# Feed-forward: T forms and the weights of the 256-column products at other columns, with one low block per run placed 64 bytes ahead

## The chip, the cores and the metric

The kernel runs on one core of a Trainium2 chip. The metric is the device time of one execution in microseconds (us). All inputs start in the chip's memory and the output ends there.

## What is computed

The reference is a two-layer encoder trunk in float32 on x of 512 x 1024. Each layer has a mixer (attention in layer 0, mLSTM in layer 1), a memory cross-attention and a gated feed-forward; a last RMS norm follows. The change touches the feed-forward alone:

```python
def conv_ffn(xn, w_up, conv_w, conv_b, w_down):
    h = causal_depthwise_conv(xn @ w_up, conv_w) + conv_b
    g, u = jnp.split(h, 2, axis=-1)
    return (jax.nn.gelu(g) * u) @ w_down
```

`w_up` is 1024 x 5632 and `w_down` 2816 x 1024. `w_up` is cut into 22 pairs of 128-column blocks: block p of g and block p of u.

## The kernel before, in words

**Three products for one.** Every float32 operand is split into a high part (rounded to the format that TensorE multiplies at full rate) and a low part (what is left). `mm3` (L271) forms one product as three matmuls into one bank: low-by-high of the moving side last. In the profile L274 is wh by xh, L275 is wh by xl, and L276 is wl by xh. The high part is made by ScalarE (`scalar.copy`), the low part by VectorE (`sub`, L264 and L265, a subtraction raw minus high).

**The feed-forward** (`ffn_steps`) goes through the 22 pairs. Pairs 0 to 3 (`plain`, L1290) use 512-column matmuls: 8 blocks of the contraction for g, 8 for u. Pairs 4 to 21 (`seven`, L1309) use a Strassen-Winograd scheme: the two halves of the contraction, the two halves of the 512 tokens and the pair's two blocks make a 2 x 2 by 2 x 2 product, done in seven products of 4 contraction blocks and 256 columns each instead of eight. Three of them (p1, p2, p3) take columns of the normal input x as the moving operand: the **X products**. Four (p4 to p7) take sums of x that are formed once per layer in `forms` (L1222) and kept split in the tiles th0 to th3 and tl0 to tl3 (L1216): the **T forms**, and the **T products**. A product is 4 blocks x 3 matmuls = 12 matmuls. The two layers have 36 such pairs, so 36 x 84 = 3024 matmuls of 256 columns, 1296 of them with X and 1728 with T.

The weights of the seven products are f3 (1024 columns, for p1 and p2), f1 (1024, for p5 and p7), s2 (512, p6), s4 (512, p3) and a22 (512, p4). `split` (L1331) makes their parts: one copy on ScalarE, one subtraction on VectorE. f1 and f3 take tiles wh and wl of 1088 columns from a rotating pool (`parts`, L251); f3 starts OFF = 16 columns, or 64 bytes, into its tile. s2, s4 and a22 have tiles of their own. Unused tiles (`pad`) push others on: 192 bytes ahead of the T forms (L1215), 64 bytes ahead of s4 (L1328).

**Where the operands lie.** All operands start at a multiple of 64 bytes. The question of this case is whether that multiple is even (a multiple of 128 bytes) or odd (64 bytes past one). In the addresses that the program before assigns, with the moving operand named first and the weights second: X products (even, odd), T products (odd, even), all 512-column products (even, even).

**The order of the work.** A small list scheduler (`Sched`, L141) holds one queue for each engine. Tasks carry a duration, dependencies, slots and a due time; the scheduler replays them and calls their functions in its order, which is the order in which the instructions are issued; a framework below it may still interleave neighbouring tasks. PE's order puts the seven products in the order p1, p6, p5, p2, p7, p3, p4, and between them, through `fill` (L1424), blocks of the second matrix (`down`, L1411): 12 matmuls of 512 columns, two or so for each pair. A **run** below means consecutive 256-column products with no 512-column block between them.

VectorE makes in each pair the low parts, two sums of weights (L1340, L1346), five sums of products (L1380), one scaling (L1401), four convolution taps (L1263), the gated product (L1273) and the addition of a down block to x (L495).

Of the kernel before, what the change touches and what calls it, by code (L numbers as in the profile page):

```python
# [10 lines left out]
F32R = mybir.dt.float32r  # L11
# [5 lines left out]
P = 128  # L17
# [19 lines left out]
OFF = 16  # L37
# [24 lines left out]
class Plan:  # L62
# [70 lines left out]
class Task:  # L133
    def __init__(self, eng, dur, fn, deps, prio, take, free, lat):
# [2 lines left out]
        self.take, self.free = take, free  # L137
        self.end = None


class Sched:  # L141

# [20 lines left out]
    def run(self):  # L163
        order = sorted(self.tasks, key=lambda t: (t.prio, t.n))
# [7 lines left out]
        now = {e: 0.0 for e in todo}  # L172
        inf = float("inf")
        idle = 0.0
        while any(todo.values()):
            best = None
            for e, ts in todo.items():
# [34 lines left out]
                st["_" + r] = s  # L212
            for r, st in t.free:
                self.slots[r][st["_" + r]] = t.end + 0.1
            if t.fn:
                t.fn()
        self.now, self.idle = now, idle


class Builder:  # L220
# [22 lines left out]
    def bank(self, tag):  # L243
        tag, bufs = BANKS[tag]
        return self.til(self.aux, tag, bufs=bufs)
# [22 lines left out]
        self.nc.scalar.copy(hi, v)  # L268
        self.sub(lo, v, hi)

    def mm3(self, out, wh, wl, xh, xl, first, last, parts=False):  # L271

        mm = self.nc.tensor.matmul
        mm(out, wh, xh, start=first, stop=False, skip_group_check=parts)  # L274
        mm(out, wh, xl, start=False, stop=False, skip_group_check=parts)  # L275
        mm(out, wl, xh, start=False, stop=last, skip_group_check=parts)  # L276
# [841 lines left out]
    def ffn_steps(self, layer, mp):  # L1118
# [36 lines left out]
        def parts(st, off=0):  # L1155
            st["wh"], st["wl"] = self.parts(off)
# [60 lines left out]
        formed, pads = [], []  # L1217
# [91 lines left out]
        def seven(p, fill):  # L1309
# [14 lines left out]
            l1 = load(a22, "ra", A2[:, 512:], 512, at - 6.0)  # L1324

            def small(s, tag):
                if tag == "s4" and not pads:
                    pads.append(self.pad(mp, 64))  # L1328
                s["wh"], s["wl"] = (self.til(mp, tag + i, (P, 512), F32R, bufs=1) for i in "hl")

            def split(s, cols, deps, due, alloc, take, raw, free=()):  # L1331
                def hi():
                    alloc()
                    nc.scalar.copy(s["wh"][:, :cols], raw())

                h = add("ACT", act(cols), hi, deps, due - 3.0, take)
                return add("DVE", tt(cols), lambda: self.sub(s["wl"][:, :cols], raw(), s["wh"][:, :cols]), [h], due - 2.0, (), free)
# [5 lines left out]
            w3 = split(f3, 1024, [l2], at, lambda: parts(f3, OFF), [("h", f3)], lambda: r2["raw"][:])  # L1343
            w2 = split(s2, 512, [b2], at, lambda: small(s2, "s2"), [("s2", s2)], SB)
            w1 = split(f1, 1024, [b1], at + 1.0, lambda: parts(f1), [("h", f1)], lambda: sa["sa"][:])
            b4 = add("DVE", tt(512), lambda: tt_(out=SB(), in0=SB(), in1=r2["raw"][:, 512:], op=ALU.add), [w2], at - 1.5)  # L1346
            w22 = split(a22, 512, [l1], at + 4.0, lambda: small(a22, "a22"), [("a22", a22)], lambda: a22["ra"][:], [("ra", a22)])
            w4 = split(s4, 512, [b4], at + 5.0, lambda: small(s4, "s4"), [("s4", s4)], SB, [("sb", sb)])
# [19 lines left out]
            p1 = pe(n, lambda: opened("X", bx, "acc", f3, 0, *X(0, 0), "X", True), [w3], [("acc", bx)])  # L1368
            p6 = pe(n, lambda: opened("Y", by, "acc", s2, 0, *T2, "Y", True), [w2, *formed], [("acc", by)], [("s2", s2)])
            p5 = pe(n, lambda: opened("R", br, "s", f1, 512, *T1, "R", True), [w1], [("s", br)])  # L1370
            get = rows(st, at + 2.0)

            def v_():
# [3 lines left out]
            def sum_(tag, out, a, b, op):  # L1377
                if tag:
                    st[tag] = self.til(mp, tag, (P, 256), bufs=1)
                tt_(out=out(), in0=a(), in1=b(), op=op)  # L1380
# [4 lines left out]
            v = add("ACT", act(256), v_, [p1], at + 1.5, [("v", bv)])  # L1385
            u2 = add("DVE", 0.34, lambda: sum_("u2", tmp("u2"), bank("Y"), tmp("v_"), ALU.add), [p6, v], at + 4.0, [("u2", bu2)])
            p2 = pe(n, lambda: product(f3, 512, *X(1, 0), "X", False), [p1, v], (), [("h", f3)])
            c11 = add("ACT", act(256), lambda: nc.scalar.copy(hs(0, 0)(), bank("X")()), [p2, get], clock[0] + 2.0, (), [("acc", bx)])
            p7 = pe(n, lambda: product(f1, 0, *T3, "Y", False), [u2, p5], (), [("h", f1)])
            u3 = add("DVE", 0.34, lambda: sum_("u3", tmp("u3"), bank("Y"), tmp("v_"), ALU.add), [p7], clock[0], [("u3", bu3)])  # L1390
            c22 = add("DVE", 0.34, lambda: sum_(None, hs(1, 1), tmp("u3"), bank("R"), ALU.subtract), [u3, p5, get], clock[0], (), [("u3", bu3)])
            fill()
            p3 = pe(n, lambda: product(s4, 0, *X(1, 1), "R", False), [c22, w4], (), [("s4", s4)])
            c12 = add("DVE", 0.34, lambda: sum_(None, hs(0, 1), bank("R"), tmp("u2"), ALU.subtract), [p3, get], clock[0], (), [("s", br), ("u2", bu2)])
            p4 = pe(n, lambda: product(a22, 0, *T4, "Y", False), [u3, w22], (), [("a22", a22)])
            c21 = add("DVE", 0.34, lambda: sum_(None, hs(1, 0), bank("Y"), tmp("v_"), ALU.add), [p4, get], clock[0], (), [("acc", by), ("v", bv)])
            fill()

# [416 lines left out]
```

## Time and profile before

| | |
|---|---|
| median of 3 executions | 1494.97 us (1494.59 to 1495.11) |
| the profiled execution | 1494.89 us, of which 1493.1 us is the span from the first to the last instruction |
| granted TensorE clock, mean | 0.999 |
| PE, busy | 1480.1 us (99%), 8570 instructions |
| VectorE (DVE), busy | 1209.5 us (81%), 2291 instructions |
| ScalarE (ACT), busy | 815.7 us (55%) |
| first `seven` pairs to the last, layer 0 and layer 1 | about 460 to 716 us and 1181 to 1437 us of the span |

A time in a profile line is in us from the span's start. The start of a matmul is recorded, its end is modelled, so the distance from one start to the next is what counts; "mean ns" of a matmul group is the modelled length from start to end, which is longer than that distance because matmuls overlap in the array.

### The profile page before, as it was taken

How to read it: one execution, taken by the hardware profiler on the slowest of the kernel's cores; microseconds unless marked ns; L12 is line 12 of the kernel's file. 1: busy time of each engine (PE TensorE's matmuls, PEld its weight loads, DVE VectorE, ACT ScalarE, POOL GpSimd, SP SyncE). 2: the span in 40 equal slices, each digit the busy share in tenths (PEclk: the TensorE clock that was granted, in tenths of full speed). 3: DMA queues.
4: the chain of work that ended last, by engine and by line, in shares of the span. 5: the costliest groups of instructions: out<-in, count | busy, mean ns of one | idle time of the engine just before them, and what ended most of it. 6: DMA issues, size and time to landing. Idle time of an engine off the chain costs nothing.

```text
span 1493.1 us, 22741 instructions
## 1 busy us (share of the span) xinstructions
PE 1480.1 (99%) x8570; PEld 1283.7 (86%) x8570; DVE 1209.5 (81%) x2291; ACT 815.7 (55%) x1369; POOL 61.4 (4%) x104
## 2 busy tenths in 40 slices
PE   9999999999999999999999999999999999999998
PEld 7888777888889999999888778888888899999987
DVE  7779795666689999999868857666566999999984
ACT  7777573444466555556446634444444655555654
POOL 0000130000001000000000000000000000000000
PEclk9999999999999999999999999999999999999999
DMA  5212223323237665562222222223323656565422
GB/s 195 85 59 82 86 84 115 127 72 127 81 131 191 168 155 157 148 162 76 91 97 85 71 99 85 99 91 121 114 72 126 179 156 170 153 158 160 108 74 75
DMA packets 62461, 174.92 MB, mean 117 GB/s; under 512 B 6800, under 2 KB 6800, under 8 KB 62352
## 3 DMA queue, kind: packets, MB, share of 16 engines
q1 hardware_dynamic: 56160, 153.48, 31.4%
q0 software_dynamic: 5184, 18.88, 7.5%
q8 instruction: 67, 1.10, 0.3%
q10 hardware_dynamic: 1008, 1.12, 0.2%
q14 instruction: 42, 0.34, 0.1%
HBM read 171.35 MB, written 2.10 MB: 116 GB/s over the span
## 4 chain that ended last, share of the span: by engine, by line
PE 90%; DVE 6%; ACT 2%; issue 1%; DMA 0%; SPq 0%; DVEq 0%; ACTq 0%
PE acc L274 18%; PE acc L276 18%; PE acc L275 18%; PE w L276 5%; PE w L274 5%; PE w L275 5%; PE s L274 3%; PE acc L335 2%; PE s L276 2%; PE acc L337 2%; PE acc L336 2%; PE s L275 2%; PE w L1603 1%; DVE wl L265 1%; PE s L401 1%
## 5 line engine op out<-in xcount | busy, mean ns | idle before, releaser
L274 PE MATMUL acc<-xh,wh 128*128 128x512 f32 (+1 forms) x800 | 285.1, 357 | 0.0
L276 PE MATMUL acc<-xh,wl 128*128 128x512 f32 (+1 forms) x800 | 280.8, 351 | 0.0
L275 PE MATMUL acc<-xl,wh 128*128 128x512 f32 (+1 forms) x800 | 280.5, 351 | 0.0
L265 DVE TENSOR_TENSOR wl<-raw,wh 128x1024 fp32r<-128x1024 f32 (+2 forms) x197 | 235.5, 1195 | 42.9 <-ACT wh L268 39.7
L268 ACT CAST wh<-raw 128x1024 fp32r<-128x1024 f32 (+2 forms) x137 | 140.6, 1029 | 164.0 <-PE acc L275 97.7
L275 PEld LDWEIGHTS acc<-xl,wh 128*128 128x128 f32 x800 | 151.3, 189 | 19.7
L276 PEld LDWEIGHTS acc<-xh,wl 128*128 128x128 f32 x800 | 150.2, 188 | 20.2
L274 PEld LDWEIGHTS acc<-xh,wh 128*128 128x128 f32 x800 | 150.2, 188 | 19.8
L1263 DVE SCALAR_TENSOR_TENSOR c<-hs,vec,c 128x512 f32<-128x512 f32 x176 | 129.7, 745 | 0.5
L274 PE MATMUL w<-ah,wh 128*128 128x512 f32 x304 | 119.1, 392 | 0.2
L276 PE MATMUL w<-ah,wl 128*128 128x512 f32 x304 | 118.7, 390 | 0.3
L275 PE MATMUL w<-al,wh 128*128 128x512 f32 x304 | 118.6, 390 | 0.0
L1256 ACT ACTIVATE c<-hs,vec 128x512 f32<-128x512 f32 x88 | 70.4, 813 | 40.5 <-DVE hs L1401 38.0
L276 PEld LDWEIGHTS w<-ah,wl 128*128 128x128 f32 x304 | 57.1, 188 | 12.7 <-DVE wl L265 0.9
L274 PEld LDWEIGHTS w<-ah,wh 128*128 128x128 f32 x304 | 57.1, 188 | 12.2 <-ACT wh L1165 1.5
L275 PEld LDWEIGHTS w<-al,wh 128*128 128x128 f32 x304 | 57.1, 188 | 10.0
L1165 ACT CAST wh<-dr 128x512 fp32r<-128x512 f32 x64 | 39.6, 618 | 45.3 <-PE acc L275 19.2
L274 PE MATMUL acc<-mem,wh 128*128 128x256 f32 (+1 forms) x192 | 61.5, 320 | 0.0
L276 PE MATMUL acc<-mem,wl 128*128 128x256 f32 (+1 forms) x192 | 61.1, 318 | 0.0
L275 PE MATMUL acc<-mem,wh 128*128 128x256 f32 (+1 forms) x192 | 60.8, 317 | 0.0
L495 DVE TENSOR_TENSOR x<-acc,x 128x512 f32<-128x512 f32 x32 | 22.1, 690 | 46.9 <-PE acc L276 46.9
L495 DVE TENSOR_TENSOR x<-w,x 128x512 f32<-128x512 f32 x72 | 49.2, 683 | 12.6 <-PE w L276 12.5
(373 smaller groups left out, 3948.2 us busy)
## 6 DMA issues: line engine op xcount, KB each, us to landing
raw<-in_up_dram SPq DMA_DIRECT2D x52, 512.0 KB, 3.3
sa<-in_up_dram SPq DMA_DIRECT2D x36, 512.0 KB, 4.1
sa<-in_up_dram POOLq DMA_DIRECT2D x36, 512.0 KB, 5.9
dr<-in_down_dram SPq DMA_DIRECT2D x64, 256.0 KB, 2.9
ra<-in_up_dram SPq DMA_DIRECT2D x36, 256.0 KB, 2.8
raw<-in_xk_dram SPq DMA_DIRECT2D x16, 512.0 KB, 3.4
raw<-in_wo_dram SPq DMA_DIRECT2D x16, 512.0 KB, 3.3
raw<-in_xq_dram SPq DMA_DIRECT2D x16, 512.0 KB, 3.3
```

The lines of the kernel that those rows point to most:

```text
L265: self.nc.vector.tensor_tensor(out=lo, in0=v, in1=hi.bitcast(F32), op=ALU.subtract)
L268: self.nc.scalar.copy(hi, v)
L274: mm(out, wh, xh, start=first, stop=False, skip_group_check=parts)
L275: mm(out, wh, xl, start=False, stop=False, skip_group_check=parts)
L276: mm(out, wl, xh, start=False, stop=last, skip_group_check=parts)
L335: mm(ps, xh[k][:, ts], wh[:, ws], start=(k == 0), stop=False)
L336: mm(ps, xh[k][:, ts], wl[:, ws], start=False, stop=False)
L337: mm(ps, xl[k][:, ts], wh[:, ws], start=False, stop=(k == 7))
L495: self.nc.vector.tensor_tensor(out=self.x[m][:], in0=ps[:], in1=self.x[m][:], op=ALU.add)
L1165: nc.scalar.copy(st["wh"][:, :cols], st[tag][:, :cols])
L1256: nc.scalar.activation(st["c_"][:, j, :], hs()[:, j, 2:514], AF.Identity, scale=self.col("cw", (layer * 3 + 2) * 44 + blk), bias=self.col( ...
L1263: nc.vector.scalar_tensor_tensor(out=c, in0=hs()[:, j, n : n + 512], scalar=w, in1=c, op0=ALU.mult, op1=ALU.add)
```

## The change

- The tiles move. The 192 bytes ahead of the T forms go, so th and tl now start at even multiples of 64 bytes. s2, a22 and s4 are allocated once per layer, behind them, with pads that put them at odd multiples. f1 gets the same 64-byte offset as f3. All seven products are then (even, odd).
- The low tiles of s2, a22 and s4 grow by 64 columns.
- The scheduler first fixes its order, then goes through PE's tasks: the first 256-column product of every run is marked.
- In a marked product one block of the low weights lies apart, at an even multiple: the first block 64 bytes ahead of its place, or the last block 192 bytes past it where the product uses the second half of a tile. In the built program 52 products are marked: 50 of the first kind (22 of p1, 22 of p3, 6 of p7) and 2 of p2 with the last block. In the first kind the blocks are multiplied in the order 1, 2, 0, 3, in the second in the order 0, 1, 3, 2, so the block set apart always comes third, and of its three matmuls the one with the low weights comes first.
- The subtraction that makes such a low part is cut in two, since its output is no longer in one piece. In the built program VectorE has 52 more instructions, 26 in each layer; all other engines have as many as before.

The core of the diff:

```diff
+        shifted = False
+        for t in done:
+            if t.eng == "PE":
+                if t.form:
+                    if not shifted:
+                        t.form[0].setdefault("shift", set()).add(t.form[1])
+                    shifted = True
+                else:
+                    shifted = False
...
+        if low:
+            mm(out, wl, xh, start=False, stop=False, skip_group_check=parts)
+            mm(out, wh, xh, start=False, stop=False, skip_group_check=parts)
+            mm(out, wh, xl, start=False, stop=False, skip_group_check=parts)
+            return
...
-        self.pad(mp, 192)
...
+        small_ = lambda tag, i: self.til(mp, tag + i, (P, 512 + 64 * (i == "l")), F32R, bufs=1)
+        for i in "lh":
+            for tag in ("s2", "a22", "s4"):
+                small_(tag, i)
+            self.pad(mp, 64 if i == "l" else 128)
...
+            def whole(s):
+                s["wh"], s["wl"] = (self.til(self.wp, i, (P, 1088), F32R, bufs=3) for i in ("wh", "wl"))
+                s["wh"] = s["wh"][:, OFF:]
+
+            def at_(s, c):
+
+                shift = s.get("shift", ())
+                return 0 if c == 0 and 0 in shift else 960 if c == 896 and 512 in shift else OFF + c
...
+                def lo():
+                    shift = s.get("shift", ())
+                    cuts = sorted({0, cols} | ({P} if 0 in shift else set()) | ({896} if 512 in shift else set()))
+                    for a, b in zip(cuts, cuts[1:]):
+                        self.sub(s["wl"][:, at_(s, a) : at_(s, a) + b - a], raw()[:, a:b], s["wh"][:, a:b])
...
-            w1 = split(f1, 1024, [b1], at + 1.0, lambda: parts(f1), [("h", f1)], lambda: sa["sa"][:])
+            w1 = split(f1, 1024, [b1], at + 1.0, whole, [("h", f1)], lambda: sa["sa"][:])
...
-                for k in range(4):
-                    w = slice(c + k * P, c + (k + 1) * P)
-                    self.mm3(st[bank][:, :256], s["wh"][:, w], s["wl"][:, w], xh(k), xl(k), first and k == 0, k == 3, True)
+                moved = c in s.get("shift", ())
+                apart = None if not moved else 0 if c == 0 else 3
+                order = (0, 1, 2, 3) if not moved else (1, 2, 0, 3) if c == 0 else (0, 1, 3, 2)
+                for n, k in enumerate(order):
+                    w, a = slice(c + k * P, c + (k + 1) * P), at_(s, c + k * P)
+                    wh, wl = s["wh"][:, w], s["wl"][:, a : a + P]
+                    self.mm3(st[bank][:, :256], wh, wl, xh(k), xl(k), first and n == 0, n == 3, True, k == apart)
```

More of the change, by code (lines that the diff above doesn't have):

```diff
@@ L138, in __init__ @@
         self.end = None
+        self.form = None
 class Sched:
@@ L174, in run @@
         idle = 0.0
+        done = []
         while any(todo.values()):
@@ L214, in run @@
                 self.slots[r][st["_" + r]] = t.end + 0.1
+            done.append(t)
+        self.now, self.idle = now, idle
+        shifted = False
[7 more added lines that the diff above has]
+                    shifted = False
+        for t in done:
             if t.fn:
                 t.fn()
-        self.now, self.idle = now, idle
 class Builder:
@@ L269, in split, with mm3 @@
         self.sub(lo, v, hi)
-    def mm3(self, out, wh, wl, xh, xl, first, last, parts=False):
+    def mm3(self, out, wh, wl, xh, xl, first, last, parts=False, low=False):
         mm = self.nc.tensor.matmul
+        if low:
[3 more added lines that the diff above has]
+            return
         mm(out, wh, xh, start=first, stop=False, skip_group_check=parts)
@@ L1326, in small @@
             def small(s, tag):
-                if tag == "s4" and not pads:
-                    pads.append(self.pad(mp, 64))
-                s["wh"], s["wl"] = (self.til(mp, tag + i, (P, 512), F32R, bufs=1) for i in "hl")
+                s["wh"], s["wl"] = small_(tag, "h"), small_(tag, "l")
+            def whole(s):
[4 more added lines that the diff above has]
+                return 0 if c == 0 and 0 in shift else 960 if c == 896 and 512 in shift else OFF + c
             def split(s, cols, deps, due, alloc, take, raw, free=()):
                 def hi():
-                    alloc()
+                    alloc(s)
                     nc.scalar.copy(s["wh"][:, :cols], raw())
+                def lo():
[3 more added lines that the diff above has]
+                        self.sub(s["wl"][:, at_(s, a) : at_(s, a) + b - a], raw()[:, a:b], s["wh"][:, a:b])
                 h = add("ACT", act(cols), hi, deps, due - 3.0, take)
-                return add("DVE", tt(cols), lambda: self.sub(s["wl"][:, :cols], raw(), s["wh"][:, :cols]), [h], due - 2.0, (), free)
+                return add("DVE", tt(cols), lo, [h], due - 2.0, (), free)
             def s2_():
@@ L1393, in seven @@
             p3 = pe(n, lambda: product(s4, 0, *X(1, 1), "R", False), [c22, w4], (), [("s4", s4)])
+            p3.form = s4, 0
             c12 = add("DVE", 0.34, lambda: sum_(None, hs(0, 1), bank("R"), tmp("u2"), ALU.subtract), [p3, get], clock[0], (), [("s", br), ("u2", bu2)])
             p4 = pe(n, lambda: product(a22, 0, *T4, "Y", False), [u3, w22], (), [("a22", a22)])
+            p4.form = a22, 0
             c21 = add("DVE", 0.34, lambda: sum_(None, hs(1, 0), bank("Y"), tmp("v_"), ALU.add), [p4, get], clock[0], (), [("acc", by), ("v", bv)])
```

15 lines of the change are left out of this document (10 added, 5 removed).

## Prediction

> **What bounds the kernel now.** I read the page's busy shares first, then the groups of instructions with their shapes kept apart, then PE in order of time, and last VectorE by windows and in the chain that ended last.
>
> ```profile
> span 1493.1 us, 22741 instructions
> PE 1480.1 (99%) x8570; PEld 1283.7 (86%) x8570; DVE 1209.5 (81%) x2291; ACT 815.7 (55%) x1369; POOL 61.4 (4%) x104
> ```
>
> PE is busy almost without a gap, so a change of PE's pace reaches the end unless another engine holds PE up. The pace is read from starts. PE in order of time, columns start and modelled length, first around a T product that follows 512-column work:
>
> ```profile
> 541.30 0.28 PE L274 MATMUL acc<-th,wh 128*128 128x256 f32 x1
> ...
> 542.72 0.39 PE L274 MATMUL w<-ah,wh 128*128 128x512 f32 x1
> ...
> 545.44 0.28 PE L274 MATMUL acc<-th,a22h 128*128 128x256 f32 x1
> ```
>
> Twelve 512-column matmuls take 545.44 - 542.72 = 2.72 us, 226.7 ns each. Twelve of 256 columns take 1.42 us, 118.3 ns each, where half of 226.7 would be 113.3. Next an X product after 512-column work, then two T products behind it, then X again:
>
> ```profile
> 569.02 0.28 PE L274 MATMUL acc<-xh,wh 128*128 128x256 f32 x1
> ...
> 570.43 0.29 PE L274 MATMUL acc<-th,s2h 128*128 128x256 f32 x1
> ...
> 571.02 0.28 PE L276 MATMUL acc<-th,s2l 128*128 128x256 f32 x1
> ...
> 571.81 0.28 PE L274 MATMUL s<-th,wh 128*128 128x256 f32 x1
> ...
> 573.17 0.28 PE L274 MATMUL acc<-xh,wh 128*128 128x256 f32 x1
> ...
> 574.59 0.29 PE L274 MATMUL acc<-th,wh 128*128 128x256 f32 x1
> ```
>
> X: 1.41 us for 12, 117.5 each. The first five T matmuls take 0.59 us, 118.0 each; the 12 from 571.81 take 1.36 us, 113.3 each; the X product from 573.17 takes 1.42 us again. So one shape has two paces, which I call **slow** (117.7, between the 117.5 and 118.3 of these rows) and **fast** (113.3), and a pace lasts until something ends it: the T product after 512 columns stayed slow to its end, the T product after X became fast. X is (even, odd) and T is (odd, even), so at that point both places flip. The modelled lengths carry the same mark:
>
> ```profile
> L276 PE MATMUL acc<-xh,wl 128*128 128x256 f32 x288 | 80.8, 281 | 0.0
> L274 PE MATMUL s<-xh,s4h 128*128 128x256 f32 x144 | 41.1, 285 | 0.1
> L274 PE MATMUL acc<-th,a22h 128*128 128x256 f32 x144 | 40.5, 281 | 0.0
> L274 PE MATMUL acc<-th,wh 128*128 128x256 f32 x144 | 40.4, 280 | 0.0
> L274 PE MATMUL acc<-th,s2h 128*128 128x256 f32 x144 | 40.1, 278 | 0.0
> L276 PE MATMUL acc<-th,s2l 128*128 128x256 f32 x144 | 39.9, 277 | 0.0
> L274 PE MATMUL s<-th,wh 128*128 128x256 f32 x144 | 39.8, 276 | 0.0
> ```
>
> Means of one: 276 is all fast, 281 all slow. X lies at 281 and above, so it is slow. The five T rows average (281 + 280 + 278 + 277 + 276) / 5 = 278.4; leaning to the matmuls with the low parts, which start no product, I take 278, or 40% slow: 113.3 + 0.4 x 4.4 = 115.1 ns. PE's 256-column matmuls now cost 1296 x 117.7 + 1728 x 115.1 = 152.5 + 198.9 = 351.4 us.
>
> The second engine to watch is VectorE. Busy time by windows over 240 us of each layer's `seven` pairs (columns: length, then PE, PEld, DVE, ACT, POOL with instruction counts), and two of the 20 us windows:
>
> ```profile
> 460.00:700.00 240.00, 239.77 (x1738) 225.63 (x1737) 234.87 (x370) 134.74 (x211) 13.70 (x16) 1.00 0.58 153
> 1181.00:1421.00 240.00, 239.85 (x1738) 225.74 (x1737) 234.70 (x370) 134.95 (x211) 13.72 (x16) 1.00 0.58 153
> ```
>
> ```profile
> 560.00:580.00 20.00, 20.00 (x137) 18.42 (x136) 18.32 (x28) 10.65 (x15) 0.85 (x1) 1.00 0.53 142
> ...
> 660.00:680.00 20.00, 19.86 (x147) 18.41 (x146) 19.94 (x34) 13.06 (x21) 0.86 (x1) 1.00 0.62 142
> ```
>
> VectorE has 5.1 to 5.3 us free in 240, and unevenly: 1.68 us free in one window, 0.06 in another. Where it is full it already sets the end. The chain that ended last runs through it from 655 to 675.6 us, up to a PE matmul that had waited:
>
> ```profile
> 655.28 0.63 ACT s2h L1334
> 655.93 0.70 DVE s2l L265
> ...
> 674.93 0.61 DVE wl L265
> 675.58 0.50 PE w L276
> ```
>
> **The change part by part.** The profiled execution took 1494.89 us (span 1493.1), 0.08 under the median of 1494.97; I sum against 1494.89.
>
> 1. *All seven products become (even, odd).* This removes the flip from X to T behind which T turned fast. Without the last part, nothing in a run would flip, and X behind 512 columns starts slow. Alone this step costs 1728 x (117.7 - 115.1) = 4.5 us.
>
> 2. *The low block set apart.* The trace of before has no matmul whose weights alone change place within a run of X or T, so this price is bounded from both sides. Upper bound of the gain: each run turns fast behind its seventh matmul and stays so. One row set says that X can be fast: a p3 behind 512 columns in which one step hesitated.
>
> ```profile
> 678.00 0.28 PE L274 MATMUL s<-xh,s4h 128*128 128x256 f32 x1
> 678.12 0.29 PE L275 MATMUL s<-xl,s4h 128*128 128x256 f32 x1
> 678.25 0.28 PE L276 MATMUL s<-xh,s4l 128*128 128x256 f32 x1
> 678.37 0.28 PE L274 MATMUL s<-xh,s4h 128*128 128x256 f32 x1
> ...
> 679.38 0.28 PE L274 MATMUL acc<-th,a22h 128*128 128x256 f32 x1
> ```
>
> Steps of 0.12, 0.13, 0.12, then nine in 1.01 us, about 113 each. So (even, odd) holds the fast pace once something has moved the weight loads against the matmuls by a few ns. The block set apart does to the weight load under way what the flip at 570.43 does: even weights are loaded while an even operand streams. It differs in what follows, since the moving side stays even. I take the value at that nearest row. Then a run costs 6 x 4.4 ns for its slow start and 5 x (118.0 - 113.3) = 24 ns for the turn, 50 ns; 52 runs cost 2.6 us, and 3024 x 113.3 = 342.6, together 345.2 us. Against 351.4 the gain is 6.2 us, 3.1 in each layer. Other end: no run turns, 3024 x 117.7 = 355.9, a loss of 4.5 us, and up to 52 x 24 ns = 1.2 us more for steps that hesitate in vain.
>
> 3. *52 more VectorE instructions.* Their price is the fixed part of a subtraction, from VectorE in order of time:
>
> ```profile
> 530.30 1.22 DVE L265 TENSOR_TENSOR wl<-sa,wh 128x1024 fp32r<-128x1024 f32 x1
> 531.43 0.42 DVE L1380 TENSOR_TENSOR u<-acc,v 128x256 f32<-128x256 f32 x1
> 531.77 0.68 DVE L265 TENSOR_TENSOR al<-c,ah 128x512 fp32r<-128x512 f32 x1
> 532.37 0.41 DVE L1380 TENSOR_TENSOR hs<-u,s 128x256 f32<-128x256 f32 x1
> ```
>
> From start to start 1024 columns take 1.13 us and 512 take 0.60, so 1.035 ns a column and 0.07 us fixed. 26 cuts in a layer are 1.8 us. They are hidden while VectorE has room, and stand in the path where it has none.
>
> 4. *Moved tiles, wider tiles, tiles allocated once.* No data move and no DMA is added; PE, ScalarE, SyncE and GpSimd have as many instructions as before, and the loads keep their order. Cost nothing, with the reuse of s2, a22 and s4 waiting for the same readers as before.
>
> *What VectorE takes back.* In a layer PE gives 3.1 us and the cuts add 1.8, together 4.9 of the 5.1 us free. In total that fits; in place it doesn't. The full windows must pass at VectorE's pace: a PE that is 1.3% quicker waits at their end. Lower end of the loss: the stretch of the chain above, 20 of 240 us, about a tenth of the gain, 0.6 us. Upper end: everything, so that both layers keep their length or lengthen by the cuts. Half of the 240 us looks like the window at 660, so I take half: 3.1 us back.
>
> Sum: 1494.9 - 6.2 + 3.1 = **1491.8 us**.
>
> A rule speaks against any effect of places. The Trainium skill ("TensorE: Matmul & The Clock Gate", section "Step-by-step: what each phase is for") says that PE reads the moving operand and the weights through two independent ports, so that loading the next weights takes no bandwidth from the running matmul. The two paces of one shape at a granted clock of 1.00 disagree with it; by it only the cuts would remain (rival C).
>
> **The rivals.**
>
> A. *The block doesn't turn the run.* For it: the one flip seen changed the moving side too, and the matmul behind it is a different pair of places; T behind 512 columns shows that a slow run stays slow by itself. Against: the turn at 678.25. Price as in 2: 1494.9 + 4.5 to 5.7, less some waits of VectorE that go: **1499.8 us**. It decides from the point where fewer than about four runs in ten turn (4.5 lost against 10.7 between the two ends).
>
> B. *It turns, and VectorE becomes the bound.* The full windows stretch over the stage, and PE's 6.2 us turn into waits at the ends of them, with some cuts added: 1494.9 - 1 = **1494 us**. For it: 4.9 of 5.1 us. Against: PE is busy for 239.77 of 240 us there, so full windows have so far hardly held it up and some buffer is left.
>
> C. *Places don't matter in this way* (the two ports' rule): 0 to 3.6 us of cuts, hidden in part: **1495.5 us**. The rows above speak against it.
>
> **How the numbers follow.** My forecast, runs that turn with VectorE giving back a tenth to nearly all, has 0.50 and runs from 1489.3 to 1494.0. A has 0.32, B 0.13, C 0.05. Cases of both signs hold much of it, so the range has to reach A: 1489.3 to 1500.3, with the likeliest case's own range beside it. 0.2% of the median is 3.0 us, about what a measurement of this kernel can tell from no change. Faster by more, under 1492.0: 0.35 of the forecast's 0.50. Slower by more, over 1498.0: A's 0.31. The rest, 0.34, is within.
>
> **What would show each step.** Right: the X groups at 276 to 277 instead of 281, T groups the same but for p7's share of starts; starts 113.3 ns apart from about the twelfth matmul of a run on; more than 1738 PE instructions in 240 us; VectorE above 236 of 240. If A: all X and T groups at 281 and starts 117.7 apart, VectorE freer than before. If B: lengths of 276, but single steps above 200 ns with VectorE ahead of them. What would make me wrong most: that the turn needs the moving side.

## The result, and the profile after

The changed kernel takes 1498.5 us (median of 11 executions, 1498.13 to 1498.80) against 1495.07 us for the kernel before (11 executions, 1494.59 to 1495.78). The ratio is 1.0022, 95% interval 1.0015 to 1.003: it is slower, by 3.4 us. The prediction was 1491.8 us, faster; its range held the time, its direction was wrong. What happened is its rival A.

The head of the page after and its chain of work, and the same line of the chain before:

```profile
span 1496.4 us, 22801 instructions
...
PE 1484.2 (99%) x8570; PEld 1288.4 (86%) x8570; DVE 1211.5 (81%) x2343; ACT 815.5 (54%) x1369; POOL 61.2 (4%) x104
...
PE 94%; DVE 3%; ACT 2%; issue 0%; DMA 0%; SPq 0%; DVEq 0%; ACTq 0%
```

```profile
PE 90%; DVE 6%; ACT 2%; issue 1%; DMA 0%; SPq 0%; DVEq 0%; ACTq 0%
```

The span grew by 3.3 us and PE's busy time by 4.1. VectorE has its 52 cuts and yet stands in the chain for 3% where it was 6%. The likely reason is that a slower PE leaves VectorE more time: e5 below, without the cuts, has 3% too. The groups by shape name the matmuls (between the two bars stand the busy us and the mean ns of one; `mm3` now begins at L286, and L295, L296, L297 stand for what L274, L275, L276 were):

```profile
L297 PE MATMUL acc<-xh,wl 128*128 128x256 f32 x264 | 73.8, 281 | 0.0
...
L297 PE MATMUL acc<-th,s2l 128*128 128x256 f32 x144 | 40.5, 281 | 0.0
...
L295 PE MATMUL s<-th,wh 128*128 128x256 f32 x144 | 40.4, 281 | 0.0
```

X stays at 281; the two T groups were at 277 and 276 and are at 281. That is the row that the prediction named for rival A. PE in order of time around one marked run (L291 to L293 are the three matmuls of the block set apart):

```profile
490.04 0.28 PE L295 MATMUL acc<-xh,wh 128*128 128x256 f32 x1
...
490.75 0.28 PE L291 MATMUL acc<-xh,wl 128*128 128x256 f32 x1
490.86 0.28 PE L292 MATMUL acc<-xh,wh 128*128 128x256 f32 x1
...
492.87 0.28 PE L295 MATMUL s<-th,wh 128*128 128x256 f32 x1
```

Six matmuls ahead of the block take 0.71 us, 118 ns each; the block's own step is 0.11, without hesitation; the 17 behind it take 492.87 - 490.86 = 2.01 us, 118 each. The run doesn't notice the block. One stretch of this kernel is fast all the same, far behind the block of its run:

```profile
472.00 0.39 PE L295 MATMUL acc<-th,a22h 128*128 128x256 f32 x1
...
473.48 0.28 PE L295 MATMUL s<-xh,s4h 128*128 128x256 f32 x1
...
474.84 0.28 PE L295 MATMUL s<-th,wh 128*128 128x256 f32 x1
```

The T matmul at 472.00 is held up (0.39 us where the others have 0.28), and the X product behind it takes 1.36 us, 113.3 each, with all operands placed as in every other run. The pace then lasts to the end of the run. So something other than places can turn a run too. Over 240 us of the first layer (columns as in the prediction):

```profile
460.00:700.00 240.00, 240.00 (x1726) 226.37 (x1725) 234.36 (x391) 133.62 (x209) 13.66 (x16) 1.00 0.58 152
```

1726 matmuls where there were 1738, at the same granted clock of 1.00, and PE without any gap.

### The profile page after: what moved, and what is told of

Its sections match the earlier page's. It is cut to its first block, busy times and chain, and to the rows that moved or that the text cites. A ratio compares the mean times of both kernels' runs of the same rounds, so it can differ in the third digit from the quotient of the medians.

```text
span 1496.4 us, 22801 instructions
## 1 busy us (share of the span) xinstructions
PE 1484.2 (99%) x8570; PEld 1288.4 (86%) x8570; DVE 1211.5 (81%) x2343; ACT 815.5 (54%) x1369; POOL 61.2 (4%) x104
## 4 chain that ended last, share of the span: by engine, by line
PE 94%; DVE 3%; ACT 2%; issue 0%; DMA 0%; SPq 0%; DVEq 0%; ACTq 0%
PE acc L295 18%; PE acc L297 18%; PE acc L296 18%; PE w L295 5%; PE w L296 5%; PE w L297 5%; PE s L295 3%; PE s L297 3%; PE s L296 3%; PE acc L356 2%; PE acc L358 2%; PE acc L357 2%; PE w L1652 1%; PE s L422 1%; PE w L925 1%; PE s L457 1%
## 5 line engine op out<-in xcount | busy, mean ns | idle before, releaser
L295 PE MATMUL acc<-xh,wh 128*128 128x512 f32 (+1 forms) x776 | 278.6, 359 | 0.0
L297 PE MATMUL acc<-xh,wl 128*128 128x512 f32 (+1 forms) x776 | 273.8, 353 | 0.0
L296 PE MATMUL acc<-xl,wh 128*128 128x512 f32 (+1 forms) x776 | 273.8, 353 | 0.0
L280 DVE TENSOR_TENSOR wl<-raw,wh 128x1024 fp32r<-128x1024 f32 (+4 forms) x221 | 237.6, 1081 | 42.9 <-ACT wh L283 39.8
L296 PEld LDWEIGHTS acc<-xl,wh 128*128 128x128 f32 x776 | 146.8, 189 | 19.6
L297 PEld LDWEIGHTS acc<-xh,wl 128*128 128x128 f32 x776 | 145.6, 188 | 20.3
L295 PEld LDWEIGHTS acc<-xh,wh 128*128 128x128 f32 x776 | 145.7, 188 | 19.8
L295 PE MATMUL w<-ah,wh 128*128 128x512 f32 x304 | 119.4, 393 | 0.3
L296 PE MATMUL w<-al,wh 128*128 128x512 f32 x304 | 118.9, 391 | 0.0
L297 PE MATMUL w<-ah,wl 128*128 128x512 f32 x304 | 118.3, 389 | 0.0
L297 PEld LDWEIGHTS w<-ah,wl 128*128 128x128 f32 x304 | 57.1, 188 | 12.2
L295 PEld LDWEIGHTS w<-ah,wh 128*128 128x128 f32 x304 | 57.1, 188 | 12.0 <-ACT wh L1186 1.1
L296 PEld LDWEIGHTS w<-al,wh 128*128 128x128 f32 x304 | 57.3, 188 | 9.9
L295 PE MATMUL acc<-mem,wh 128*128 128x256 f32 (+1 forms) x192 | 61.5, 320 | 0.0
L297 PE MATMUL acc<-mem,wl 128*128 128x256 f32 (+1 forms) x192 | 61.1, 318 | 0.0
L296 PE MATMUL acc<-mem,wh 128*128 128x256 f32 (+1 forms) x192 | 60.8, 317 | 0.0
```

Source lines behind the costliest of these rows:

```text
L280: self.nc.vector.tensor_tensor(out=lo, in0=v, in1=hi.bitcast(F32), op=ALU.subtract)
```

## The experiments

Each run is beside executions of the kernel before on the same chip (medians 1495.05 to 1495.16). The letters in the expectations are names of theories; what each expects is said there in numbers.

**Places.** The prediction described places as even or odd multiples of 64 bytes. The runs forced a finer description. Below, a place is the start in steps of 64 bytes within 256, from 0 to 3, and a pair is (moving, weights). In the addresses of the programs, the kernel before has X at (2,3), T at (1,2) and the 512-column blocks of the second matrix at (2,2). The changed kernel has X and T at (2,3), the 512 columns at (2,2) and the block set apart at (2,2). "Slow" is 117.7 ns from start to start, "fast" 113.3.

### First: e1 to e4, and a fault in them

These four were meant to change only the 256-column operands. Pads that I misplaced moved the gated activations too, the moving operand of the 512-column blocks: from place 2 to 1 (e1, e4) or 3 (e2, e3). In e2 and e3 s4's high part also lay at 1 instead of 3. So their times answer another question than they were made for; their traces answer a useful one.

**e1**: all products (2,3), nothing set apart, no cuts.

```diff
-                    if not shifted:
+                    if False:
...
-        for i in "lh":
-            for tag in ("s2", "a22", "s4"):
-                small_(tag, i)
-            self.pad(mp, 64 if i == "l" else 128)
+        self.pad(mp, 64)
+        for tag, i in [('s2', 'h'), ('s2', 'l'), ('a22', 'h'), ('a22', 'l'), ('s4', 'h'), ('s4', 'l')]:
+            small_(tag, i)
+        self.pad(mp, 64)
```

> The changed kernel with no product marked: no block set apart, no cut subtraction; all seven products (even, odd). Theory M (only the place of the moving operand decides, a block of weights set apart does nothing): all 256-column starts 117.6 ns apart, 1498.3 us. Theory V (the 52 cuts on VectorE are what costs): 1495 us. Theory A (the block does something, only too little): a change of PE's pace against the changed kernel, either way.

Measured: 1495.53 us (1495.02 to 1496.17), ratio 1.0004 [0.9995, 1.0013]. PE in order of time, the first matmul of X behind 512 columns and of the three products behind it, then a 512-column group of this kernel and the same of the kernel before:

```profile
490.56 0.28 PE L296 MATMUL acc<-xh,wh 128*128 128x256 f32 x1
...
491.93 0.28 PE L296 MATMUL acc<-th,s2h 128*128 128x256 f32 x1
...
493.29 0.28 PE L296 MATMUL s<-th,wh 128*128 128x256 f32 x1
...
494.65 0.28 PE L296 MATMUL acc<-xh,wh 128*128 128x256 f32 x1
```

```profile
L297 PE MATMUL w<-al,wh 128*128 128x512 f32 x304 | 119.9, 394 | 0.0
```

```profile
L275 PE MATMUL w<-al,wh 128*128 128x512 f32 x304 | 118.6, 390 | 0.0
```

Products of 1.37, 1.36 and 1.36 us: fast from the first one on, and without any flip or block. What differs from the changed kernel is the 512-column work ahead, now at (1,2). So the pace of a run is set by what comes before it. The 512 columns pay for it: most of their steps are 231 to 236 ns instead of 226 to 227, 79.4 us a layer instead of 77.9 (summed from the starts, from the first 256-column product of a layer to its last).

**e2**: T, its weights and its order as before; the block set apart only in runs that begin with X.

```diff
-            p6.form = s2, 0
+            p6.form = {}, 0
-            p4.form = a22, 0
+            p4.form = {}, 0
```

(likewise for p5 and p7, with the T forms and their weights at the places of the kernel before)

> The kernel before with the block set apart in the runs that begin with an X product, T forms and weights at their old places, so X (even, odd) and T (odd, even). Theory M: pace as before, T fast behind X, 1495.1 us, at most 0.5 more for the cuts. Theory V: 1497 to 1498.5 us.

Measured: 1496.23 us (1495.58 to 1496.86), ratio 1.0008 [0.9999, 1.0017].

```profile
491.26 0.28 PE L297 MATMUL acc<-xl,wh 128*128 128x256 f32 x1
491.37 0.28 PE L298 MATMUL acc<-xh,wl 128*128 128x256 f32 x1
491.49 0.28 PE L292 MATMUL acc<-xh,wl 128*128 128x256 f32 x1
...
492.19 0.28 PE L296 MATMUL acc<-th,s2h 128*128 128x256 f32 x1
```

Here X had become fast by its fifth matmul (114 ns from start to start); from the block on its six steps take 0.70 us, 117 each. The block at (2,2) does have an effect, the reverse of the one it was credited with: it ends the 113.3 ns pace.

**e3 and e4**: T moved alone. e3 has T and its weights both on odd places, e4 both on even ones.

```diff
+AT = {"s2": 0, "a22": 0, "f1": OFF, "s4": 0, "f3": OFF}
...
-                s["wh"] = s["wh"][:, OFF:]
+                s["wh"] = s["wh"][:, AT[tag] :]
```

(e3; with 192 bytes ahead of the T forms. e4 has "f1": 0 and the forms even)

> No block; T forms odd as before, but their weights odd too, so that between X and T only the moving operand flips. Theory M: T turns fast behind X as before (113.3 ns), 1495.1 us. Theory B (both sides must flip): T stays slow, 1498.5 us or more.

> No block; T forms even and their weights even, so that between X and T only the weights flip. Theory M: T stays slow, 1498.3 us, more if (even, even) has a slower pace of its own (119.8 ns in the mixer's products of that kind would give 1502). Theory W (the weights' flip decides): T fast, 1495 us. Theory B: T slow.

Measured: e3 1500.95 us (1500.68 to 1501.23), ratio 1.004 [1.0027, 1.0052]; e4 1504.66 us (1504.46 to 1505.29), ratio 1.0065 [1.0053, 1.0078]. A T group of e3, then of e4:

```profile
L296 PE MATMUL s<-th,wh 128*128 128x256 f32 x144 | 40.5, 282 | 0.0
```

```profile
L296 PE MATMUL s<-th,wh 128*128 128x256 f32 x144 | 40.8, 283 | 0.0
```

There is a third pace. From start to start T takes 119.5 ns at (1,1) and 118.5 at (1,3) in e3, and 119.8 at (2,2) in e4. The parity of the moving operand alone, or of the weights alone, is not what makes T fast.

### Second: the block by itself, with the activations in and out of place

**e5**: the changed kernel, nothing set apart; everything else where it was.

```diff
-                    if not shifted:
+                    if False:
```

> The changed kernel with every low block left in its place (no block 64 bytes ahead, no cuts): all 256-column products (even, odd), and, unlike in e1, the gated activations stay on even places, so the 512-column matmuls stay (even, even). Theory A (the block apart does nothing to a slow run; the pace is set by where the run starts): X and T at 281 ns from the first matmul of each run to the last, 117.6 apart, time 1498.4 (1498.5 less 0 to 0.2 for the 52 cuts), so 3 to 3.5 us over before. Rival M2 (the block is what breaks a fast pace here): runs get fast as in e1, X and T at 277 to 278, time 1495 or less, 3 us under the changed kernel.

Measured: 1498.92 us (1498.41 to 1499.42), ratio 1.0026 [1.0016, 1.0036].

```profile
L297 PE MATMUL acc<-th,s2l 128*128 128x256 f32 x144 | 40.5, 281 | 0.0
...
L295 PE MATMUL s<-th,wh 128*128 128x256 f32 x144 | 40.4, 281 | 0.0
```

The same T groups, to the nanosecond, as with the block, and within 0.4 us the same time (0.5 over what theory A said; M2 is out). So the block and its 52 cuts together change nothing that these times can tell, and the loss is the first part of the change: all products at (2,3).

**e6**: the changed kernel with the block, and the activations on an odd place.

```diff
-            self.pad(mp, 64 if i == "l" else 128)
+            self.pad(mp, 64)
```

> The changed kernel, block apart and cuts kept, with one pad 64 bytes shorter, so that the gated activations lie on odd places and the 512-column matmuls are (odd, even). Theory S (the pace is a state; behind (odd, even) a run of (even, odd) starts fast, and a weights-only step turns fast to slow, never slow to fast): starts at 113 to 114 ahead of the block and 117 to 118 behind it; 52 of the runs have it at their seventh matmul, so nearly everything behind is slow; 512-column steps 233 instead of 227; time 1500.5 to 1501.5 (1498.5 plus 3 for the 512s, less 0.5 for the fast starts). Rival A2 (the block does nothing in either state): as e1, 113.3 to the end of the run, 1495.5 to 1496.

Measured: 1502.2 us (1501.85 to 1502.29), ratio 1.0047 [1.0033, 1.0061].

```profile
500.35 0.28 PE L295 MATMUL s<-xh,s4h 128*128 128x256 f32 x1
...
500.69 0.28 PE L291 MATMUL s<-xh,s4l 128*128 128x256 f32 x1
...
501.40 0.28 PE L295 MATMUL acc<-th,a22h 128*128 128x256 f32 x1
...
502.81 0.40 PE L295 MATMUL w<-ah,wh 128*128 128x512 f32 x1
```

Three steps in 0.34 us ahead of the block (113 each); six in 0.71 from it on; 12 T matmuls in 1.41 (117.5). Theory S is right in kind: the run starts fast and the block ends that. The time is 0.7 us over its range.

**e7**: no block, and wider tiles for the activations, so that their places alternate.

```diff
-                acts[p] = tuple(self.til(mp, n, dtype=F32R, bufs=10) for n in ("ah", "al"))
+                acts[p] = tuple(self.til(mp, n, (P, 528), F32R, bufs=10)[:, :512] for n in ("ah", "al"))
```

(and the tiles wh and wl narrowed from 1088 to 1056 columns to make room)

> All 256-column products (even, odd), no block apart, and the tiles of the gated activations 64 bytes wider, so that they alternate between even and odd by pair and the last 512-column step ahead of a run of products is (odd, even). Theory S (behind an (odd, even) step a run of (even, odd) starts fast and stays so): 256-column steps at 114 to 115 on average as in e1, while the half of the 512-column matmuls that is (even, even) costs 227 instead of 233: time 1493.5 to 1495. Rival S2 (it takes several odd 512-column steps to set the state, or a step between even and odd costs more): runs slow, 117.6, or 512 steps above 233: 1497 to 1500.

Measured: 1502.93 us (1502.44 to 1503.41), ratio 1.0052 [1.0039, 1.0065]: a miss. A group of 512-column work on x, most of it in the mixer and the cross-attention, in this kernel, and in the changed one:

```profile
L296 PE MATMUL acc<-xl,wh 128*128 128x512 f32 x512 | 201.9, 394 | 0.0
```

```profile
L296 PE MATMUL acc<-xl,wh 128*128 128x512 f32 x512 | 199.8, 390 | 0.0
```

The kernel before has the same row as the changed one, 199.8 and 390. The 256-column steps came near what S says: 174.9 and 174.6 us a layer, 115.7 and 115.5 ns each, against 176.4 us before. The 512-column steps between them did not: they cost 1 us a layer more than before. In all a layer takes 253.7 and 253.6 us from its first 256-column product to its last, against 254.2 and 254.1 before. The loss lies outside, in the 512-column work, 2 us in this one of its groups. The narrower tiles put the rotating weight buffers 128 bytes apart within 256, so that (even, even) stayed (even, even) and yet became slower: a first sign that 128 bytes are not the period.

**e8**: the kernel before with the block in runs that begin with X, activations on an even place (the edit of e2 with other pads).

> The kernel before (X (even, odd), T (odd, even), gated activations on even places) with the block set apart in those runs alone that begin with an X product. Theory A (a weights-only step does nothing to a slow run): the marked X products stay at 117.5 from start to start on both sides of the block, T behind X gets fast at the flip as in before; time 1495.0 to 1495.6. Rival M (the weights' step moves the load as the flip does, and it failed in the changed kernel for another reason): X fast behind its seventh matmul, X groups at 277 to 279, and T behind it slow again or fast; 1493 to 1494.5, or, if the flip then turns fast T to slow, 1497 to 1498.

Measured: 1499.49 us (1498.87 to 1500.48), ratio 1.0029 [1.0018, 1.0041]. This fits neither theory, and the places are the likely reason: even, but 0 instead of 2 for the activations and 1 instead of 3 for s4's high part.

The group of e1's 512-column row has 394 here too, where the kernel before has 390, and these steps sum to 79.2 us a layer instead of 77.9. The run says nothing on the block; e10 repeats it.

### Third: every pair of places by itself

**e9** leaves the computation out. TensorE multiplies constants in the kernel's pattern of twelve, with nothing else running.

```diff
+        def product(n, pm, pw, order=range(12), at=None, other=None):
...
+            for i in order:
+                k, j = divmod(i, 3)
+                q = other if i == at else pw
+                lhs = w[j == 2][:, 16 * q + P * k : 16 * q + P * k + P]
+                rhs = m[j == 1][:, 640 * k + 16 * pm : 640 * k + 16 * pm + n]
+                mm(ps[:, :n], lhs, rhs, start=i == 0, stop=i == 11, skip_group_check=True)
```

> Leaves the whole computation out: TensorE alone multiplies constants in the kernel's pattern of twelve (four blocks, three matmuls each), with the starts of both operands set by hand; the output is zeros. Places are counted in steps of 64 bytes within 256, as (moving, weights): the kernel before has X at (2,3), T at (1,2), 512 columns at (2,2), the changed kernel all at (2,3). First each of the 16 pairs for 36 matmuls of 256 columns behind twelve of 512 at (2,2); then each pair for 24 of 512; then the block set apart in (2,3); then runs that change pair; then starts behind 512 columns at (1,2). Theory S (the pace depends on both places and on the state in which the run starts): behind (2,2) the pairs (2,3) and (1,2) are slow, 117.7, equal places about 119.8, 512 columns 226.7 at (2,2) and about 233 at (1,2); (2,3) behind (1,2) fast, 113.3; the block at (2,2) changes no step of a slow run. Rival W (the pace comes from what else runs in the kernel, VectorE's and ScalarE's use of the memory above all): all 16 pairs within 1 ns of each other.

It was executed once and took 422.6 us, at a granted clock of 0.995. Steps from start to start in ns, the mean of the second half of each stretch by the recorded starts, all behind 512 columns at (2,2):

| moving place | 256 columns, weights at 0, 1, 2, 3 | 512 columns, weights at 0, 1, 2, 3 |
|---|---|---|
| 0 | 120.0, 117.8, 120.0, 117.8 | 226.7, 233.3, 233.3, 228.9 |
| 1 | 117.8, 120.0, 117.8, 118.6 | 228.9, 226.7, 233.3, 232.7 |
| 2 | 120.0, 117.8, 120.0, 117.8 | 232.6, 228.8, 226.7, 233.3 |
| 3 | 117.8, 120.0, 117.8, 120.0 | 233.3, 232.6, 228.8, 226.7 |

In the main the distance between the two places decides, within 256 bytes. For 512 columns no distance is best, and the sign counts: weights one place behind the moving operand cost 228.8 to 228.9, one place ahead 233.3. For 256 columns no distance is worst, and 128 bytes are as bad except at (1,3). Now the runs that change pair. Of each stretch one row: start, length to the modelled end of the last, count. The pace is (length - 0.28) / (count - 1):

```profile
110.84 2.87 PE L1740 MATMUL acc<-ops 128*128 128x256 f32 x23
...
278.20 3.23 PE L1740 MATMUL acc<-ops 128*128 128x256 f32 x26
...
285.53 2.77 PE L1740 MATMUL acc<-ops 128*128 128x256 f32 x23
...
292.05 3.23 PE L1740 MATMUL acc<-ops 128*128 128x256 f32 x26
```

The first is (2,3) throughout, 2.59 / 22 = 117.7. The others are (2,3) behind one step to (2,2), to (2,1) and to (2,0): 118.0, then 2.49 / 22 = **113.2**, then 118.0. A weights-only step can turn the pace from 117.7 to 113.3, but of the three places tried in a (2,3) run only place 1 does it, 128 bytes from where the run's weights lie. At 64 bytes, as in the change, nothing happens. The other turns: (1,2) behind a slow (2,3); (2,3) behind a slow (1,2); (1,2) behind a fast (2,3); (2,3) behind (2,1); (2,3) behind 512 columns at (1,2); (2,3) fast, behind one step to (2,2):

```profile
335.00 2.09 PE L1740 MATMUL acc<-ops 128*128 128x256 f32 x17
...
351.42 2.40 PE L1740 MATMUL acc<-ops 128*128 128x256 f32 x19
...
359.54 2.64 PE L1740 MATMUL acc<-ops 128*128 128x256 f32 x21
...
376.42 2.66 PE L1740 MATMUL acc<-ops 128*128 128x256 f32 x22
...
399.04 3.56 PE L1740 MATMUL acc<-ops 128*128 128x256 f32 x30
...
406.38 3.23 PE L1740 MATMUL acc<-ops 128*128 128x256 f32 x26
```

113.1, 117.8, 118.0, 113.3, 113.1, 118.0. The first is the turn at 570.43 of the prediction; the last is e2's and e6's. The third is new: the flip from (2,3) to (1,2) turns 117.7 into 113.3, but also 113.3 into 117.7. The kernel before has that too: the T product at 679.38, behind the X product that got fast at 678.25, takes 118 ns a step. Rival W is out: no other engine was busy then, and the 16 pairs lie between 117.8 and 120.0 ns, not within 1.

**e10**: e8's question with every place right to 256 bytes.

```diff
+        self.pad(mp, 64)
+        for tag, i in [('s2', 'h'), ('s2', 'l'), ('a22', 'h'), ('a22', 'l'), ('s4', 'l')]:
+            small_(tag, i)
+        self.pad(mp, 64)
+        small_("s4", "h")
+        self.pad(mp, 128)
```

> As e8, with the places kept to 256 bytes: X (2,3), T (1,2), 512 columns (2,2) exactly as in the kernel before, and the block set apart at (2,2) in the 23 runs that begin with an X product, the cuts for it on VectorE. In e2 and e8 the gated activations and s4's high part lay 64 or 128 bytes off by 256, and the 512-column steps were at 230 to 233. Theory A (the block does nothing to a slow run): X steps 117.5 on both sides of the block, T behind X fast at the flip as before, 512 steps 227, time 1495.0 to 1495.8. Rival M (the block turns runs): X at 277 to 279 and 1493 to 1494.5; rival D (the block spoils the flip that follows, as e8's time could say): T 1 ns slower, 1496.5 to 1499.

Measured: 1494.3 us (1493.94 to 1494.6), ratio 0.9994 [0.9985, 1.0003].

```profile
490.54 0.28 PE L296 MATMUL acc<-xh,wh 128*128 128x256 f32 x1
...
491.25 0.28 PE L292 MATMUL acc<-xh,wl 128*128 128x256 f32 x1
...
491.96 0.29 PE L296 MATMUL acc<-th,s2h 128*128 128x256 f32 x1
...
493.34 0.28 PE L296 MATMUL s<-th,wh 128*128 128x256 f32 x1
...
494.70 0.28 PE L296 MATMUL acc<-xh,wh 128*128 128x256 f32 x1
```

0.71 us for the six ahead of the block, 0.71 from it on, then the flip and 1.38 and 1.36 for T. The block does nothing to matmuls 117.7 apart, theory A, and leaves the flip alone, against D. The time is 0.7 us under A's range and 0.8 under the kernel before, within the interval. By the starts that does not come from the products: their 256-column steps sum to 176.3 and 176.4 us a layer, as in the kernel before (176.4 in both).

**e11**: no block, and the weights of all seven products at place 1.

```diff
+AT = 48
...
-                s["wh"] = s["wh"][:, OFF:]
+                s["wh"] = s["wh"][:, AT:]
```

(with 128 bytes ahead of the small tiles)

> The changed kernel without the block and its cuts, and with the weights of all 256-column products 64 bytes behind the 512-column ones instead of 64 ahead: all seven (2,1), 512 columns (2,2) as before. Theory S, with the sign taken from e7 (256-column steps at (2,1) there were 113.8 and 114.7 on average): runs start fast behind (2,2) and stay so, 256-column steps 113.5 to 114.5, sum per layer 174 to 175 of 176.4 with some waits for VectorE as in e1, 512 steps 227: 1491 to 1493.5, faster than both kernels. Rival (only the distance of 64 bytes counts, not its sign): slow as in e5, 1498.4 to 1499.

Measured: 1498.3 us (1497.97 to 1499.14), ratio 1.0023 [1.0014, 1.0031].

```profile
460.00:700.00 240.00, 239.95 (x1725) 226.16 (x1724) 233.42 (x367) 133.74 (x209) 13.66 (x16) 1.00 0.59 152
```

1725 matmuls in 240 us, as slow as the changed kernel. S's sign was wrong and the rival right. e9 agrees, 117.8 at (2,1) behind 512 columns at (2,2). That e7's (2,1) steps were fast because their runs already were is likely, but nothing here has (2,1) alone behind products at 113.3.

### Fourth: the block 128 bytes ahead

**e12**: the changed kernel, and only the place of the block set apart is different: (2,1).

```diff
-                return 0 if c == 0 and 0 in shift else 960 if c == 896 and 512 in shift else OFF + c
+                return 0 if c == 0 and 0 in shift else 960 if c == 896 and 512 in shift else s.get("off", 32) + c
```

(with the tiles of wl and s4's low part starting 64 bytes earlier within 256, so that their other columns stay at place 3)

> The changed kernel with one difference: the low block that is set apart lies 128 bytes ahead of its place instead of 64, so that its one matmul is (2,1), counted in steps of 64 bytes within 256, instead of (2,2). All other operands of TensorE stay at the places of the changed kernel, with the same 52 products and the same cuts. Theory S, with e9's row (one step to (2,1) in a slow run of (2,3): 121, 116, 114, 114, then 113.3 to the end; to (2,2) nothing): the 52 marked runs turn behind their seventh matmul and stay fast, X and T groups at 276 to 278 instead of 281, 256-column steps of a layer 172.2 without waits (1512 of 113.3, and 26 slow starts of 30 ns) and 173 to 175 with VectorE's waits: 1489 to 1492, faster than both kernels. Rival B (they turn, but VectorE gives nearly all back): groups at 276 to 278, waits of 3 us and more in a layer, 1493 to 1496. Rival A2 (the turn seen in e9 needs a memory that no other engine uses): 1498.5, as the changed kernel.

Measured: **1492.11 us** (1491.68 to 1492.7), ratio to the kernel before 0.998 [0.9971, 0.9989]; 6.4 us under the changed kernel.

```profile
490.43 0.28 PE L307 MATMUL acc<-xh,wh 128*128 128x256 f32 x1
...
491.13 0.28 PE L303 MATMUL acc<-xh,wl 128*128 128x256 f32 x1
...
491.48 0.28 PE L307 MATMUL acc<-xh,wh 128*128 128x256 f32 x1
...
491.82 0.28 PE L307 MATMUL acc<-th,s2h 128*128 128x256 f32 x1
...
493.18 0.28 PE L307 MATMUL s<-th,wh 128*128 128x256 f32 x1
```

Slow up to the block (0.70 us for six), then three steps in 0.35 us, three in 0.34 and T's twelve in 1.36: fast to the end of the run. By the starts, 49 of the 52 marked runs turn at their block. Two were fast from the start and stay fast through it; one, at 545.35 us, stays slow. The groups, the window and the chain:

```profile
L309 PE MATMUL acc<-xh,wl 128*128 128x256 f32 x264 | 72.9, 277 | 0.0
...
L309 PE MATMUL acc<-th,s2l 128*128 128x256 f32 x144 | 39.8, 276 | 0.0
```

```profile
460.00:700.00 240.00, 239.59 (x1751) 225.05 (x1750) 236.54 (x396) 136.14 (x213) 13.68 (x16) 1.00 0.58 153
```

```profile
PE 87%; DVE 9%; issue 2%; ACT 1%; DMA 0%; DVEq 0%; ACTq 0%
```

276 to 277, 1751 matmuls where there were 1726, VectorE at 236.5 of 240 us, and 9% of the chain instead of 3%: these are the rows that the prediction had named as the signs of its forecast. The turn of the runs stands, and rival A2 falls. The time lies 0.1 us over S's range and 0.9 under B's.

## Why the prediction was wrong

**Step 1, all seven (even, odd): right, a little too dear.** Priced at 4.5 us alone; e5 is this step alone, 1498.92 - 1495.13 = 3.8 us. T's groups went to 281 as said. The price left out what PE no longer waits for: the chain's share of VectorE fell from 6% to 3%.

**Step 2, the low block set apart: this failed.** "The block set apart does to the weight load under way what the flip at 570.43 does: even weights are loaded while an even operand streams." And then: "I take the value at that nearest row." The gain side was taken, 6.2 us, where the end with no turn was right: the block's own effect is nothing, 1498.5 us with it and 1498.92 without (e5). Even and odd were too coarse a description. The flip goes from (2,3) to (1,2) and stays there; the block goes to (2,2) and back, and e5, e9 and e10 show three times that this changes no step where matmuls are 117.7 apart. What turns one is (2,1), which in the prediction's own words is (even, odd) like its neighbours, no change at all. In its seven products and the blocks between them the kernel before had only the pairs (2,3), (1,2) and (2,2), so its trace could not tell a period of 128 bytes from one of 256. The second support, the turn at 678.25, shows only that (2,3) can be fast. No weights changed place there: the 512-column work ahead of it had been held up at 675.58 and its steps were still 224 to 236 ns, and the changed kernel's turn behind 472.00 also follows a held-up matmul. Why a run that was held up turns, no run here shows.

**Step 3, the cuts: hidden, as it allowed.** With them and the block 1498.5, without both 1498.92: nothing, in a kernel where PE leaves VectorE more time.

**Step 4, moved tiles at nothing: right for this change, wrong as a rule.** Here all operands outside the seven products keep their places. In e1, e4 and e8 the activations moved by 64 or 128 bytes, and the median of their 512-column steps went from 227 to 232 or 233. In e7, with weight buffers 128 bytes apart, the work outside the feed-forward's `seven` pairs cost some 9 us more (7.8 in the median and 1.0 that the two layers' pairs had gained).

**What VectorE takes back: about right, seen in e12.** There the runs turn, and the gain over the kernel before is 1495.16 - 1492.11 = 3.05 us, where the prediction had 6.2 - 3.1 = 3.1. Half of 6.2 was a guess between two ends, so that the sizes meet is in part luck. By the starts, the 256-column steps of a layer sum to 174.9 and 174.8 us in e12; with 1512 steps of 113.3 and 26 slow starts of 30 ns (1.05 us for the nine up to 491.48 instead of 1.02) they would be 172.1. So 2.7 to 2.8 us in each layer go to steps that were held up and to what is slow behind them. The prediction gave back only 1.6, but it also set out too low: its 351.4 us for the two layers are 352.8 by the starts of the kernel before, which has held-up steps as well.

**Rivals.** A happened, at 1498.5 instead of 1499.8: its steps "that hesitate in vain" cost nothing (0.11 us at 490.75), and VectorE's waits shrank. B did not come to the test in the change, since nothing turned. In e12 it does: 22 of the 256-column steps are over 200 ns, where the kernel before has 12, which is B's sign, but the time is 1492.1, under its 1494. C is refuted: e9 has one shape at 113.3, 117.8 and 120.0 ns by nothing but the two starts and what ran ahead. The Trainium skill ("TensorE: Matmul & The Clock Gate", section "Step-by-step: what each phase is for") has two independent ports for the moving operand and the weights. What the prediction drew from that for rival C doesn't hold here: with the moving operand at place 2, the 512-column steps of e9 go from 226.7 to 233.3 ns as the weights go from place 2 to place 3. What in the memory or the array makes the difference, no run here shows.

## What to carry to other kernels

A pace that depends on where operands lie must be described by the period that the chip uses, and a trace with only two or three pairs of places can't give it: measure the full table of pairs, by itself, before building on one of them. Where a stage's matmuls have two paces, look at what turns one into the other: here a single step 128 bytes off did, one 64 bytes off didn't. Whoever moves a tile for one reader moves all tiles behind it: compare every operand's place before and after, not only those that were meant.

## What the runs showed of the hardware that was not expected

- The steps of 256 and of 512 columns depend on the distance between the two starts within 256 bytes, in opposite ways (e9): at no distance 120.0 and 226.7 ns, at 64 bytes 117.8 (or 113.3) and 228.8 to 233.3.
- At (2,3) and at (1,2) the 256-column pace has two states, 117.7 and 113.3, that last until something turns them. In e9 (2,3) behind (2,1) turned fast, (2,1) behind a slow (2,3) stayed slow, the flip from (2,3) to (1,2) turned either state into the other, and (2,2) for one step turned fast to slow and not slow to fast.
- A run can also turn behind a matmul that was held up: slow to fast in the changed kernel behind 472.00 us, fast to slow in e12 behind steps of 540 and 222 ns at 471.74 and 472.28 us.
- In e9 512 columns at (1,2), 233.3 ns each, leave a following (2,3) run fast, and at (2,2), 226.7 each, leave it slow: the cheaper neighbour makes the dearer run.
